# Norm factors return as broadcasts from DRAM instead of through transposes and matmuls on TensorE

## The chip, the core and the metric

The kernel runs on one core of one Trainium2 chip. A core has five engines with a queue of instructions each: TensorE (PE in the profile, its weight loads as PEld), VectorE (DVE), ScalarE (ACT), GpSimd (POOL) and SyncE (SP), which here issues almost all DMAs. Each engine runs its queue in order, and semaphores order the engines among themselves. PE reads SBUF and writes PSUM; a [128, 512] float32 tile of PSUM is one bank. The metric is the device time of one execution in microseconds. Times below come from the median of three timed runs and from one profiled execution.

## The reference

Two layers of a decoder trunk over 528 tokens (16 learned meta tokens, then 512), width 1024, batch 1, all in float32:

```python
for l in range(DEPTH):                                   # DEPTH = 2
    h = rmsnorm(h_res, norm_gain[l])
    proj = h @ w_in[l]
    u_pool, z_pool, c_q, c_kv, k_rope, z_mla, g_pool, g_mla = jnp.split(proj, IN_SPLIT_POINTS, axis=-1)
    y_pool = (pool_mix(u_pool, ...) * jax.nn.silu(z_pool)) @ pool_w_up[l]
    o_mla = mla(c_q, c_kv, k_rope, pos, ...)
    y_mla = (o_mla * jax.nn.silu(z_mla)) @ mla_w_up[l]
    merged = jax.nn.sigmoid(g_pool) * y_pool + jax.nn.sigmoid(g_mla) * y_mla
    h_res = h_res + merged @ w_out[l]
return h_res[:, N_META:]
```

`rmsnorm` divides each token's vector by the root of its mean square plus 1e-6. Inside `mla` the latents `c_q` (768 wide) and `c_kv` (256) are normalized in this way, then the queries and keys of 8 heads (96 wide, of which 32 are rotary) are computed from them, normalized per head and token, and used in causal softmax attention. Three sets of norm factors matter here: one per token for the residual stream, one per token for `c_kv`, and eight per token (one a head) for the keys.

## The kernel before

**Layout.** Tokens lie along the free dimension: an activation is a set of [128 features, 528 tokens] tiles. A norm factor, one number per token, must multiply all 128 partitions of such a tile, so it is needed as a [128, 528] tile with equal rows. The norms are applied late: the residual stream is multiplied by its gain and used as it is, and what leaves a projection is multiplied by the token's factor when it is evicted from PSUM.

**Products.** Each float32 product is made of three passes: operands are split into a rounded part (`hi`, float32r) and the rest (`lo`), and `mm3` (L179) issues hi x hi, hi x lo and lo x hi. Weights come in chunks of [128, 512]: `wload` (L165) loads one into a `raw` buffer from SP, ACT rounds it into `whi` (L175) and DVE subtracts it into `wlo` (L176). There are three buffers each of `raw`, `whi` and `wlo`, so a load waits until an earlier chunk has been converted, and a conversion until PE has used an earlier one.

**Order.** All weight products of both layers stand in one list, `plan`, made by `register` (L911). `stream` (L187) is a generator that emits them in this order, a few matmuls at a time, with an estimated cost. `go` (L977) writes the rest of the layer by hand and draws from this stream in between: `up(name)` emits until a product is done, `fill_now(ns)` (L264) emits products worth so many estimated ns. In the attention heads, `gap` (L974) does the same between scores, softmax and value products until a reserve is reached, so that PE always has independent products to work on. A scheduler then fixes each engine's order; PSUM tiles of the tag `mm` rotate through four banks.

**The start.** ACT issues the load of the first weight chunk; SP issues the gains, then x in five parts with three weight chunks between (L122 to L125), then the constants and the positions. PE runs ten matmuls on a tile of ones (L138). `split_h` (L329) makes `hh` and `hl` of a 128-feature slice of x, `square_x` (L336) its squares; the first projections `ckv0` and `ckv1` run over the slices as they come.

**Token norms.** `norm_sums` (L340) sums the squares of x and of `c_kv` over the partitions by matmuls with ones (L348), transposes the sums so that tokens lie along the partitions (L360, L361) and computes the inverse roots by three Newton steps on DVE (`newton`, L283) into `ninv`, [128, 2, 5]: factor, then four blocks of 128 tokens and one of the meta tokens. To come back along the free dimension, the factors are split in a rounded part and a rest and padded into a tile `v`; `rows` (L387) transposes it block by block on PE (L389, L391, L392) and ACT copies it out of PSUM into `kinv`; `spread` (L273) multiplies it with a selector, which sums the two parts and copies the row to 128 partitions (L276), and ACT copies the result into `self.inv` and `self.cinv`. The first is used by the evictions of `u`, `zp`, `zm`, `gp`, `gm` and of the rotary key, the second by those of the keys `k0` to `k3`.

**Key norms.** `qk_stats` (L638) does the same with the sums of squares of queries and keys, 16 per token: transposes (L657, L658), Newton into `ny` [128, 5, 16], then for two groups of four heads padding, `rows` (five transposes and two copies) and a DMA of four rows to DRAM (`kdr`, L685). `spread_k` (L692) loads a row back as a broadcast to 128 partitions (`bc`, three buffers). `prep` (L696) multiplies the keys of a head by it on DVE and POOL (L703, L704) and splits the product into `kh` and `kl` on ACT and DVE (L270, L271), which the scores of `head` (L717) read.

Of the kernel before, what the change touches and what calls it, by code (L numbers as in the profile page):

```python
# [9 lines left out]
F32 = mybir.dt.float32  # L10
F32R = mybir.dt.float32r
# [46 lines left out]
WARM = 10  # L58
# [13 lines left out]
def trunk(ctx, tc, xT, pos, win, wkr, wqb, wkb, wvb, wgr, wpu, wmu, wout, gains, const, yT):  # L72
# [26 lines left out]
    def mmt():  # L99
        return pp.tile([P, 512], F32, tag="mm", name=nm("mm"), bufs=4)  # L100
# [12 lines left out]
    def fetch(src, n, raw, eng):  # L113
        eng.dma_start(raw[:, :n], src)
        return raw

    def rawt():
        return wp.tile([P, 512], F32, tag="raw", name=nm("raw"), bufs=3)

    early.append(fetch(win[0, MT_CKV, :, 0:512], 512, slot("rinv"), act))  # L120
    sp.dma_start(gn, gains)
    for k0, k1, m, c in ((0, 1, 1, 0), (1, 2, None, 0), (2, 4, 0, 1), (4, 6, 1, 1), (6, 8, None, 0)):  # L122
        sp.dma_start(xb[:, k0:k1, :T], xT[:, k0:k1, :])
        if m is not None:
            early.append(fetch(win[0, MT_CKV + m, :, 512 * c:512 * c + 512], 512, rawt(), sp))  # L125
    xt = [xb[:, k] for k in range(8)]
    sp.dma_start(cst, const)
# [4 lines left out]
    sp.dma_start(posb[:, :T], pos.partition_broadcast(P))  # L132
# [8 lines left out]
    dve.tensor_copy(maskw[:, 512 - P:], cst[:, C_MASK:C_MASK + P])  # L141
    kinv = cp.tile([34, T], F32R, name="kinv")
    sel = cp.tile([64, 2], F32R, name="sel")
    gp.memset(sel.bitcast(F32), 0.0)
    for i in range(2):
        gp.memset(sel[32 * i:32 * i + 2, i:i + 1].bitcast(F32), 1.0)
    identr = cp.tile([P, P], F32R, name="identr")
    dve.tensor_copy(identr, ident)
# [30 lines left out]
    def mm3(out, wh, wl, xh, xl, start, stop):  # L179
        pe.matmul(out, wh, xh, start=start, stop=False)  # L180
        pe.matmul(out, wh, xl, start=False, stop=False)  # L181
        pe.matmul(out, wl, xh, start=False, stop=stop)  # L182

    plan = []
# [88 lines left out]
    def spread(dst, i):  # L273
        for a, b in FULL:
            ps = mmt()[:, :b - a]
            pe.matmul(ps, sel[0:34, i:i + 1].to_broadcast([34, P]), kinv[:, a:b], start=True, stop=True)  # L276
            act.activation(dst[:, a:b], ps, AF.Copy)

# [28 lines left out]
    kdr = [[dp.tile([4, T], F32, name=f"kdr{l}{s}") for s in range(2)] for l in range(DEPTH)]  # L307
# [3 lines left out]
    class Layer:  # L311
        def __init__(self, l):
            self.l, self.last = l, l == DEPTH - 1
            self.XS = XTOK if self.last else FULL
            self.x0 = NM if self.last else 0
            self.xt = xt if l == 0 else [None] * 8
            self.hs, self.us, self.zps = hbuf, [None] * 4, [None] * 4
            self.cs, self.cqs, self.ys, self.am = [None] * 2, [None] * 6, [None] * 4, [None] * 8
            self.kn, self.qn, self.zms, self.ogs = [None] * 4, [None] * 4, [None] * 4, [None] * 4
            self.qr, self.qf = [None] * 2, [None] * 2  # L320
            self.gms, self.mg, self.xr, self.vw = [None] * 8, [None] * 8, [None] * 8, []
            self.csq, self.xsq = [None] * 2, [None] * 8
            self.sq, self.nsq, self.asq = [], [0, 0], 0
            self.st = self.acc = self.inv = self.cinv = self.kraw = self.kp = None
# [4 lines left out]
        def split_h(self, k):  # L329
            gk, x = self.g(G_H + k), self.xt[k]  # L330
            hh, hl = self.hs[k]
            act.activation(hh[:, :T], x[:, :T], AF.Copy, scale=gk)
            dve.scalar_tensor_tensor(out=hl[:, :T], in0=x[:, :T], scalar=gk, in1=hh[:, :T].bitcast(F32),
                                     op0=ALU.mult, op1=ALU.subtract)

        def square_x(self, k):  # L336
            self.xsq[k] = slot(f"cq{4 + k}" if k < 4 else f"q{k}")
            act.activation(self.xsq[k][:, :T], self.xt[k][:, :T], AF.Square)

        def norm_sums(self):  # L340
# [30 lines left out]
            w = tmp()  # L371
            gp.memset(w[:, 0:170], 0.0)
            v = w[:, 0:170].rearrange("p (j c) -> p j c", c=34)
            nv = ny.rearrange("p a j -> p j a")
            nh = sm.tile([P, 5, 2], F32R, tag="nh", name=nm("nh"))
            dve.tensor_copy(nh, nv)
            dve.tensor_copy(v[:, :, 0:33:32], nh.bitcast(F32))
            dve.tensor_sub(v[:, :, 1:34:32], nv, nh.bitcast(F32))
# [8 lines left out]
        def rows(self, v, n, out):  # L387
            kt1, kt2 = mmt(), mmt()
            pe.transpose(kt1[0:n, 0:NM], v[0:NM, 4, :], ident[0:NM, 0:NM])  # L389
            for j in range(3):  # L390
                pe.transpose(kt1[0:n, NM + P * j:NM + P * (j + 1)], v[:, j, :], ident)  # L391
            pe.transpose(kt2[0:n, 0:P], v[:, 3, :], ident)  # L392
            c1 = NM + 3 * P
            act.activation(out[0:n, 0:c1], kt1[0:n, 0:c1], AF.Copy)
            act.activation(out[0:n, c1:T], kt2[0:n, 0:P], AF.Copy)
# [242 lines left out]
        def qk_stats(self):  # L638
# [35 lines left out]
            ws = []  # L674
            for s in range(2):
                w = tmp()
                gp.memset(w, 0.0)
                v = w[:, 0:485].rearrange("p (j c) -> p j c", c=97)
                dve.tensor_copy(v[:, :, 0:97:32], ny[:, :, 4 * s:4 * s + 4])
                ws.append(v)  # L680
# [11 lines left out]
        def spread_k(self, h):  # L692
            self.bcs[h] = bc = slot("bc", bufs=3)
            sp.dma_start(bc, kdr[self.l][h // 4][h % 4:h % 4 + 1, :].partition_broadcast(P))
# [216 lines left out]
        def register(self, nxt):  # L911
# [17 lines left out]
            for m in range(3):  # L929
                cq(m)  # L930
# [11 lines left out]
            cq(3)  # L942
# [8 lines left out]
            cq(4)  # L951
            y(3)
            cq(5)
# [23 lines left out]
        def go(self, nxt):  # L977
            l = self.l
            up = lambda name: upto((l, name))
            if l == 0:  # L980
                for k in range(8):
                    if k in (0, 1, 3, 5):
                        step()
                    self.split_h(k)
            up("ckv1")
# [4 lines left out]
            up("u0")  # L990
# [7 lines left out]
            up("cq3")  # L998
# [7 lines left out]
            fill_now(2600)  # L1006
            kq = self.prep(0)
            fill_now(2600)
# [102 lines left out]
```

## Time and profile before

| | us |
|---|---|
| median of 3 runs | 802.42 |
| lowest, highest | 802.06, 803.46 |
| the profiled execution | 803.0 |
| its span, first to last instruction | 801.2 |
| PE busy | 793.5 |
| DVE busy | 527.8 |
| ACT busy | 417.0 |
| POOL busy | 196.2 |

A row of a timeline has the start in us from the span's start, the time in us, the engine, the source line, the operation, out<-in by the program's names, the shape and the count of like instructions merged, and in brackets idle time of the engine and what ended it. The chain of waits has start, length and what; its shares say where the chain that ended last was. Matmuls are pipelined, so that one takes longer than the distance to the next; their starts show the rate. In the view of waits a row has the waiting instruction, what it waited for, us in total, how often and the longest. In the table of queues a row has packets, MB and the time that the packets took as a share of 16 DMA engines over the stretch.

### The profile page before, as it was taken

The numbers are of one execution on the slowest core, as the hardware profiler recorded it, in microseconds if no ns is written. First come the engines' busy times: TensorE is split into PE (matmuls) and PEld (weight loads), VectorE is DVE, ScalarE is ACT, GpSimd is POOL, SyncE is SP. The second block draws the span as 40 slices with busy tenths as digits, with TensorE's granted clock in tenths as the row PEclk, the third lists the DMA queues.
The fourth block names the chain that finished last, engine by engine and source line by source line (L and its number), as shares of the span: only waits on it lengthen the run. The fifth ranks groups of instructions, "written<-read, shape, count | busy, mean of one in ns | idle before, by whom it ended". The sixth has DMA issues, their size and how long they took to land.

```text
span 801.2 us, 14644 instructions
## 1 busy us (share of the span) xinstructions
PE 793.5 (99%) x5343; PEld 715.1 (89%) x5343; DVE 527.8 (66%) x1139; ACT 417.0 (52%) x946; POOL 196.2 (24%) x266
## 2 busy tenths in 40 slices
PE   9999999999999999999999999999999999999998
PEld 8889999999999999999997897877788888887887
DVE  5568767437689887685354686665467889664942
ACT  7455645545556665543254456445455666644421
POOL 1024404103433322142000164032024333410600
PEclk9999999999999999999999999999999999999999
DMA  6222233324222222224642222324242322222272
GB/s 240 73 64 96 73 100 91 109 83 140 86 87 87 78 69 67 83 89 143 181 142 73 73 87 86 98 81 119 85 157 90 101 84 79 68 78 69 92 227 102
DMA packets 48872, 80.71 MB, mean 101 GB/s; under 512 B 5904, under 2 KB 14480, under 8 KB 48800
## 3 DMA queue, kind: packets, MB, share of 16 engines
q1 hardware_dynamic: 48656, 79.52, 32.3%
q8 instruction: 42, 0.69, 0.4%
q14 instruction: 30, 0.25, 0.1%
q10 hardware_dynamic: 144, 0.26, 0.1%
HBM read 73.40 MB, written 4.23 MB: 97 GB/s over the span
## 4 chain that ended last, share of the span: by engine, by line
PE 95%; DMA 2%; ACT 1%; DVE 1%; issue 0%; POOL 0%; SPq 0%; ACTq 0%; POOLq 0%
PE mm L180 28%; PE mm L182 27%; PE mm L181 27%; PE mm L798 2%; PE S L180 2%; PE S L181 2%; PE S L182 2%; PE o L804 1%; PE o L803 1%; PE mm L348 1%; PE S L457 1%; DMA raw<-wmu 1%; DMA xb<-xT 1%; DMA bc<-kdr 1%; PE mm L415 0%
## 5 line engine op out<-in xcount | busy, mean ns | idle before, releaser
L180 PE MATMUL mm<-hh,whi 128*128 128x264 f32 (+2 forms) x1096 | 346.3, 318 | 0.2 <-ACT racc L812 0.2
L181 PE MATMUL mm<-hl,whi 128*128 128x264 f32 (+2 forms) x1096 | 343.5, 314 | 0.0
L182 PE MATMUL mm<-hh,wlo 128*128 128x264 f32 (+2 forms) x1096 | 342.2, 315 | 0.0
L176 DVE TENSOR_TENSOR wlo<-raw,whi 128x512 fp32r<-128x512 f32 (+2 forms) x251 | 186.5, 747 | 120.1 <-ACT whi L175 112.6
L175 ACT ACTIVATE whi<-raw 128x512 fp32r<-128x512 f32 (+2 forms) x251 | 150.3, 602 | 185.9 <-PE mm L181 131.5
L180 PEld LDWEIGHTS mm<-hh,whi 128*128 128x128 f32 x1096 | 205.7, 188 | 13.5 <-ACT racc L812 0.5
L181 PEld LDWEIGHTS mm<-hl,whi 128*128 128x128 f32 x1096 | 206.2, 188 | 12.2 <-issue 0.4
L182 PEld LDWEIGHTS mm<-hh,wlo 128*128 128x128 f32 x1096 | 205.1, 188 | 12.7 <-issue 0.4
L704 POOL TENSOR_TENSOR tmp<-kp,bc 64x528 f32<-64x528 f32 x16 | 24.5, 1531 | 113.5 <-DMA bc<-kdr 78.2
L535 POOL TENSOR_TENSOR racc<-racc,tmp 128x264 f32<-128x264 f32 (+1 forms) x15 | 14.1, 942 | 143.5 <-ACT tmp L534 143.4
L776 POOL TENSOR_TENSOR pm<-pa,rs 128x16 f32<-128x16 f32 x32 | 11.6, 361 | 145.5 <-DVE rs L771 140.7
L886 POOL TENSOR_TENSOR tmp<-tmp,xb 128x264 f32<-128x264 f32 (+1 forms) x24 | 27.0, 1145 | 59.1 <-DVE tmp L884 33.7
L732 DVE CUSTOM_DVE_ANT_0 S<-S,maskw,nqs 128x272 f32<-128x272 f32 (+4 forms) x80 | 38.4, 498 | 1.6 <-PE S L182 1.2
L739 ACT ACTIVATE cq<-S,bia 128x400 f32<-128x400 f32 (+2 forms) x48 | 24.6, 516 | 21.5 <-DVE bia L766 11.6
L180 PE MATMUL mm<-u,whi 128*128 128x264 f32 (+1 forms) x108 | 35.3, 327 | 0.0
L182 PE MATMUL mm<-cq,wlo 128*128 128x264 f32 (+1 forms) x108 | 34.8, 323 | 0.0
L182 PE MATMUL mm<-u,wlo 128*128 128x264 f32 (+1 forms) x108 | 34.8, 322 | 0.0
L181 PE MATMUL mm<-cq,whi 128*128 128x264 f32 (+1 forms) x108 | 34.8, 322 | 0.0
L180 PE MATMUL mm<-cq,whi 128*128 128x264 f32 (+1 forms) x108 | 34.7, 322 | 0.0
L271 DVE TENSOR_TENSOR tl<-mm,th 128x512 fp32r<-128x512 f32 (+1 forms) x64 | 29.3, 481 | 6.8 <-ACT th L270 5.8
L778 POOL TENSOR_TENSOR cq<-cq,rs 128x384 f32<-128x384 f32 (+1 forms) x32 | 32.8, 1025 | 0.0
L180 PE MATMUL mm<-q,whi 128*128 128x264 f32 (+1 forms) x96 | 30.0, 324 | 1.0 <-ACT whi L175 0.5
(262 smaller groups left out, 1380.0 us busy)
## 6 DMA issues: line engine op xcount, KB each, us to landing
raw<-win SPq DMA_DIRECT2D x143, 256.0 KB, 2.6
raw<-wout SPq DMA_DIRECT2D x32, 256.0 KB, 3.1
bc<-kdr SPq DMA_DIRECT2D x16, 264.0 KB, 3.6
raw<-wpu SPq DMA_DIRECT2D x16, 256.0 KB, 2.7
raw<-wmu SPq DMA_DIRECT2D x16, 256.0 KB, 2.6
raw<-wqb SPq DMA_DIRECT2D x12, 256.0 KB, 2.7
tmp<-xT SPq DMA_DIRECT2D x16, 132.0 KB, 2.9
tmp<-scr SPq DMA_DIRECT2D x7, 256.0 KB, 4.7
```

The costliest lines, as they stand in the source:

```text
L175: act.activation(hi[:, :n], raw[:, :n], AF.Copy)
L176: dve.tensor_sub(lo[:, :n], raw[:, :n], hi[:, :n].bitcast(F32))
L180: pe.matmul(out, wh, xh, start=start, stop=False)
L181: pe.matmul(out, wh, xl, start=False, stop=False)
L182: pe.matmul(out, wl, xh, start=False, stop=stop)
L271: dve.tensor_sub(lo[:, a:b], src, hi[:, a:b].bitcast(F32))
L704: gp.tensor_mul(kf[r0:r0 + 64, :], self.kp[r0:r0 + 64, :], bc[r0:r0 + 64, :])
L732: dve.tensor_tensor_reduce(out=sv, in0=sv, in1=mask, scale=nqs[:, i, h:h + 1], scalar=3e38, op0=ALU.add, op1=ALU.min, accum_out=bia[:, c:c ...
L739: act.activation(pv, sv, AF.Exp, scale=-1.0, bias=bia[:, i:i + 1], accum_out=rs[:, c:c + 1])
L778: gp.tensor_mul(pt[i][:, NM:], pt[i][:, NM:], rs[:, i:i + 1].to_broadcast([P, n - NM]))
L798: pe.transpose(tr[:, P * (i - j):P * (i - j + 1)], pt[i][:, NM + P * j:NM + P * (j + 1)], ident)
L886: gp.tensor_add(t[:, :b - a], t[:, :b - a], self.am[m][:, a:b])
```

## The change

The factors leave the layout in which Newton makes them (tokens along the partitions) by DMAs that write them one element at a time into DRAM rows, `ndr` for the two token norms and `kdr` for the keys, and come back by a load that copies a row to 128 partitions. `rows`, `spread`, `kinv`, `sel` and the padding go. The load back is tied to a product: `behind` adds a wait for `newest`, the last matmul emitted by `mm3` at that point. `cq3` and `cq4` move ahead of `u0`, `cinv` gets another slot, `up("u0")` goes, `up("cq3")` becomes `up("k3")`, and the amounts of `fill_now` change. At the start, the loads of x from the third slice on, with weights between, constants and positions, wait for the landing of the first weight chunk; the first `split_h` works in halves; in layer 0 the squares of a slice wait until the slice three later has been rounded; there are eight warm-up matmuls.

```diff
-WARM = 10
+RET = 12500.0
+WARM = 8
...
-    early.append(fetch(win[0, MT_CKV, :, 0:512], 512, slot("rinv"), act))
+    early.append(slot("rinv"))
+    first = act.dma_start(early[0][:, 0:512], win[0, MT_CKV, :, 0:512])
     sp.dma_start(gn, gains)
-    for k0, k1, m, c in ((0, 1, 1, 0), (1, 2, None, 0), (2, 4, 0, 1), (4, 6, 1, 1), (6, 8, None, 0)):
-        sp.dma_start(xb[:, k0:k1, :T], xT[:, k0:k1, :])
-        if m is not None:
-            early.append(fetch(win[0, MT_CKV + m, :, 512 * c:512 * c + 512], 512, rawt(), sp))
+    sp.dma_start(xb[:, 0, :T], xT[:, 0, :])
+    early.append(fetch(win[0, MT_CKV + 1, :, 0:512], 512, rawt(), sp))
+    sp.dma_start(xb[:, 1, :T], xT[:, 1, :])
...
+    def other_loads(made):
+        for k, m in ((2, 0), (4, 1), (6, None)):
+            ins = sp.dma_start(xb[:, k:k + 2, :T], xT[:, k:k + 2, :])
+            behind(ins, made)
+            if m is not None:
+                raw = rawt()
+                behind(sp.dma_start(raw, win[0, MT_CKV + m, :, 512:1024]), made)
+                early.append(raw)
+        behind(sp.dma_start(cst, const), made)
+        behind(sp.dma_start(posb[:, :T], pos.partition_broadcast(P)), made)
...
     def mm3(out, wh, wl, xh, xl, start, stop):
...
-        pe.matmul(out, wl, xh, start=False, stop=stop)
+        newest[0] = pe.matmul(out, wl, xh, start=False, stop=stop)
...
-    def spread(dst, i):
-        for a, b in FULL:
-            ps = mmt()[:, :b - a]
-            pe.matmul(ps, sel[0:34, i:i + 1].to_broadcast([34, P]), kinv[:, a:b], start=True, stop=True)
-            act.activation(dst[:, a:b], ps, AF.Copy)
...
-    kdr = [[dp.tile([4, T], F32, name=f"kdr{l}{s}") for s in range(2)] for l in range(DEPTH)]
+    ndr = [[dp.tile([1, T], F32, name=f"ndr{l}{i}") for i in range(2)] for l in range(DEPTH)]
+    kdr = [dp.tile([H, T], F32, name=f"kdr{l}") for l in range(DEPTH)]
...
         def square_x(self, k):
...
+            if self.l == 0:
+                behind(made, self.made[min(k + 3, 7)])
...
             newton(ny, na, nt)
-            w = tmp()
-            gp.memset(w[:, 0:170], 0.0)
...
-            fill_now(8200)
-            self.rows(v, 34, kinv)
-            self.inv, self.cinv = slot("rinv"), slot("cq9")
-            fill_now(1300)
-            spread(self.inv, 0)
-            spread(self.cinv, 1)
+            self.inv, self.cinv = slot("rinv"), slot("q1")
+            for i, d in enumerate((self.inv, self.cinv)):
+                row = ndr[self.l][i]
+                sp.dma_start(row[0, NM:T].rearrange("(j p) -> p j", p=P), ny[:, i, 0:4])
+                sp.dma_start(row[0, 0:NM].rearrange("(p j) -> p j", j=1), ny[0:NM, i, 4:5])
+            fill_now(RET)
+            for i, d in enumerate((self.inv, self.cinv)):
+                behind(sp.dma_start(d[:, 0:T], ndr[self.l][i].partition_broadcast(P)), newest[0])
...
-            fill_now(9500)
-            for s, v in enumerate(ws):
-                t = tmp()
-                self.rows(v, 97, t[0:97, 0:T])
-                sp.dma_start(kdr[self.l][s], t[0:97:32, 0:T])
+            row = kdr[self.l]
+            for j in range(4):
+                sp.dma_start(row[:, NM + P * j:NM + P * (j + 1)].rearrange("h p -> p h"), ny[:, j, 0:8])
+            sp.dma_start(row[:, 0:NM].rearrange("h p -> p h"), ny[0:NM, 4, 0:8])
+            fill_now(11000)
             self.bcs = {}
             for h in range(2):
-                self.spread_k(h)
+                behind(self.spread_k(h), newest[0])
...
-            for m in range(3):
+            for m in range(5):
                 cq(m)
...
             self.norm_sums()
-            up("u0")
...
-            up("cq3")
+            up("k3")
             self.mix(3)
...
             self.qk_stats()
-            fill_now(2600)
+            fill_now(3600)
             kq = self.prep(0)
-            fill_now(2600)
+            fill_now(3600)
```

More of the change, by code (lines that the diff above doesn't have):

```diff
@@ L140, in trunk @@
     gp.memset(maskw[:, :512 - P], 0.0)
[L141 to L146, printed above, removed]
-    identr = cp.tile([P, P], F32R, name="identr")
-    dve.tensor_copy(identr, ident)
+    identr = cp.tile([P, P], F32R, name="identr")
+    def other_loads(made):
[8 more added lines that the diff above has]
+        behind(sp.dma_start(posb[:, :T], pos.partition_broadcast(P)), made)
+        dve.tensor_copy(maskw[:, 512 - P:], cst[:, C_MASK:C_MASK + P])
+        dve.tensor_copy(identr, ident)
     tcos = cp.tile([P, T], F32, name="tcos")
@@ L321, in __init__ @@
             self.gms, self.mg, self.xr, self.vw = [None] * 8, [None] * 8, [None] * 8, []
+            self.made = [None] * 8
             self.csq, self.xsq = [None] * 2, [None] * 8
@@ L693, in spread_k @@
             self.bcs[h] = bc = slot("bc", bufs=3)
-            sp.dma_start(bc, kdr[self.l][h // 4][h % 4:h % 4 + 1, :].partition_broadcast(P))
+            return sp.dma_start(bc, kdr[self.l][h:h + 1, :].partition_broadcast(P))
         def prep(self, h):
@@ L950, in register @@
             y(2)
-            cq(4)
+            cq(5)
             y(3)
-            cq(5)
             for r in range(2):
@@ L984, in go @@
                     self.split_h(k)
+                    if k == 0:
+                        other_loads(first)
             up("ckv1")
```

36 lines of the change are left out of this document (7 added, 29 removed).

## Prediction

> **What bounds the kernel now.** I read the page first: who is busy, and which engine carries the chain that ended last.
>
> ```profile
> PE 793.5 (99%) x5343; PEld 715.1 (89%) x5343; DVE 527.8 (66%) x1139; ACT 417.0 (52%) x946; POOL 196.2 (24%) x266
> PEclk9999999999999999999999999999999999999999
> PE 95%; DMA 2%; ACT 1%; DVE 1%; issue 0%; POOL 0%; SPq 0%; ACTq 0%; POOLq 0%
> ```
>
> TensorE (PE) is busy 99% of the span at full granted clock and is 95% of the chain. Since "busy" is modelled, I checked the view of waits for PE alone: its longest waits are these, each once.
>
> ```profile
> PE S L180 <- ACT kh L270: 0.6, 1, 0.6
> PE mm L276 <- ACT rinv L277: 0.5, 1, 0.5
> PE S L180 <- ACT hh L332: 0.4, 1, 0.4
> ```
>
> So the time is the sum of what PE issues plus a few waits under 1 us. Any instruction taken off PE shortens the end by its issue pitch, and a new wait of PE lengthens it one for one. Work on DVE, ACT, POOL and SP counts only where PE ends up waiting for it. This is the state in which the change has to be priced.
>
> **Part 1, what leaves PE.** The change drops 30 transposes (six calls of `rows`, five each), eight matmuls of `spread`, and two of ten warm-up matmuls. Pipelined matmuls are priced by start to start, not by their duration. The timeline of PE around the layer-0 norm rows:
>
> ```profile
> 40.41 0.28 PE L181 MATMUL mm<-hl,whi 128*128 128x264 f32 x1
> 40.53 0.28 PE L182 MATMUL mm<-hh,wlo 128*128 128x264 f32 x1
> 40.74 0.19 PE L389 MATMUL mm<-cst,tmp 16*34 16x16 f32 x1
> 40.85 0.50 PE L391 MATMUL mm<-cst,tmp 128*34 128x128 f32 x3
> 41.20 0.27 PE L392 MATMUL mm<-cst,tmp 128*34 128x128 f32 x1
> 41.22 0.37 PE L180 MATMUL mm<-hh,whi 128*128 128x264 f32 x1
> 41.43 0.28 PE L181 MATMUL mm<-hl,whi 128*128 128x264 f32 x1
> ...
> 42.28 0.28 PE L182 MATMUL mm<-hh,wlo 128*128 128x264 f32 x1
> 42.49 0.63 PE L276 MATMUL mm<-kinv,sel 34*128 34x264 f32 x3
> 43.60 0.38 PE L276 MATMUL mm<-kinv,sel 34*128 34x264 f32 x1 [0.48 <-ACT rinv L277]
> 43.91 0.39 PE L180 MATMUL mm<-hh,whi 128*128 128x264 f32 x1
> 44.14 0.28 PE L181 MATMUL mm<-hl,whi 128*128 128x264 f32 x1
> ```
>
> An ordinary 264-column matmul starts every 0.12 us (40.41 to 40.53). From 40.53 to 41.43 there would be two pitches (0.24) without the rows; it takes 0.90, so a group of five costs 0.66, the slow matmuls on both sides included. The four spreads take 44.14 - 42.28 - 0.24 = 1.62, of which 0.48 is the wait for ACT to empty a PSUM bank. The other groups by their outer rows, on the same timeline:
>
> ```profile
> 174.60 0.28 PE L182 MATMUL mm<-u,wlo 128*128 128x264 f32 x1
> ...
> 175.53 0.28 PE L181 MATMUL mm<-th,whi 128*128 128x264 f32 x1
> ...
> 176.04 0.37 PE L182 MATMUL mm<-u,wlo 128*128 128x264 f32 x1
> ...
> 177.28 0.28 PE L181 MATMUL mm<-th,whi 128*128 128x264 f32 x1
> ```
>
> ```profile
> 450.10 0.28 PE L181 MATMUL mm<-hl,whi 128*128 128x264 f32 x1
> ...
> 450.98 0.29 PE L180 MATMUL mm<-hh,whi 128*128 128x264 f32 x1
> ```
>
> ```profile
> 577.36 0.40 PE L182 MATMUL mm<-u,wlo 128*128 128x512 f32 x1
> ...
> 578.63 0.39 PE L181 MATMUL mm<-th,whi 128*128 128x512 f32 x1
> ```
>
> Key rows of layer 0: 0.93 - 0.24 = 0.69 and 1.24 - 0.24 = 1.00. Layer 1's matmuls are 512 wide, pitch 0.12 x 512/264 = 0.23, so one of its two key groups costs 1.27 - 0.46 = 0.81, both 1.62. Its norm rows I take as layer 0's, 0.66. One pair of its spreads costs 0.88 - 0.24 = 0.64, both pairs 1.28. Sum: 0.66 + 1.69 + 1.62 + 0.66 + 1.62 + 1.28 = **7.5 us**. Nothing covers this work today, PE issues it in line; the ACT and DVE copies around it are off the path and I price them at nothing.
>
> **Part 2, the return of the key norms, where the change can lose.** The chain of waits shows how keys return now:
>
> ```profile
> 177.03 1.72 DMA kdr<-tmp
> 178.77 4.78 DMA bc<-kdr
> 183.71 1.77 POOL tmp L704
> 185.50 0.65 ACT kh L270
> 186.20 0.57 PE S L180 x2
> ```
>
> From issue of the broadcast to the first scores takes 186.20 - 178.77 = 7.4 us. In the changed program the factors are written straight from their [128, 8] layout: four DMAs of 1,024 single elements and one of 128, 4,224 in all, 264 on each of 16 DMA engines. The broadcasts stand behind them on SP, waiting for their landing and for one named matmul. Let T0 be the end of the transposes of the statistics (L657/L658):
>
> ```profile
> 165.00 0.17 PE L658 MATMUL mm<-cst,tmp 16*16 16x16 f32 x1
> ```
>
> ```profile
> 169.42 0.24 DVE L290 SCALAR_TENSOR_TENSOR ny<-nt,ny 128x80 f32<-128x80 f32 x1
> ```
>
> So the factors exist 169.66 - 165.00 = 4.7 us after T0. By the changed program's order, 89 matmuls lie between T0 and the matmul that the broadcast waits for (10.7 us) and 73 more before the first scores (8.8 us, T0 + 19.5). In layer 1 it is 47 and 39 wide ones, 10.9 and 9.1 us. If the writes have landed by T0 + 10.7, kh is ready at T0 + 18.1: 1.4 us to spare, and the 0.6 us that PE waits for kh today, before the first scores (first row of the view of waits), is gone. I book **0.6 us** of gain. PE stalls only if the writes land after T0 + 12.1, which is 7.4 us after the first is issued.
>
> What does a one-element write cost? No row here shows one. The lower bound is nothing beyond today's small store, 1.72 us from issue to landing. Above, the page's queue row gives the mean packet of the kernel, mostly 2 KB long:
>
> ```profile
> q1 hardware_dynamic: 48656, 79.52, 32.3%
> ```
>
> 0.323 x 801.2 x 16 / 48,656 = 85 ns. The nearest row is the same view for the first 2.2 us, where hardly more than the 192-byte rows of the gains move on that queue:
>
> ```profile
> q1 hardware_dynamic: 58, 0.01, 3.1%
> ```
>
> 0.031 x 2.2 x 16 / 58 = 19 ns. I take 19: 264 x 19 = 5.0 us, landing 6.7 us after issue, within the 7.4; the far end, 85 ns, is 22.4 us and a stall of 22.4 + 1.7 - 7.4 = 16.7 us in each layer. So this part is 0 with little room, and the bounds are 0 and +33 us. The Trainium skill, "DMA: Bandwidth & Descriptors", Rules for kernel authors, speaks against the change: a strided last dimension becomes one descriptor per element and should be rearranged. Its section Bandwidth gives about 10.5 ns a packet; by that the estimate would be 2.8 us of engine time and the sum would stay as it is. No run here shows either yet.
>
> **Part 3, the norm return.** Only 1,056 elements in four DMAs, 66 per engine: 1.3 us at 19 ns. In layer 0 the broadcast waits for the matmul 94 pitches (11.3 us) behind its transposes, Newton included; the first reader that could hold PE (u0's eviction, whose PSUM is needed again by u1) is 139 matmuls or 16.7 us later, against 4.8 us for a broadcast. Moving cq3 and cq4 ahead of u0 makes that room. So nothing. On SP both broadcasts stand ahead of weight loads; but the first load behind them waits itself for a buffer that a later matmul frees, so the wait delays no load as long as the writes are in time. `fill_now` takes 11,000 before, and 3,600 twice in place of 2,600 around, the first head, so the heads have about 3 us less filler left; in the built order the filler still lasts into the last head in both layers. I allow **-0.3 us** for small waits at those ends.
>
> **Part 4, the start.** The first matmuls:
>
> ```profile
> 1.05 4.64 PE L138 MATMUL wps<-ones 128*128 128x128 f32 x20 [1.05 <-DVE na L662]
> ```
>
> ```profile
> 5.34 0.79 PE L180 MATMUL S<-hh,whi 128*128 128x264 f32 x2
> ```
>
> ```profile
> 2.12 5.04 DMA xb<-xT
> 7.17 0.74 ACT hh L332
> 7.96 0.51 PE S L180 x2
> ```
>
> Warm-up ends where real work starts, so eight instead of ten and a halved first split let it start up to 0.5 us sooner. The second slice of x lands at 7.16 because three more loads share the engines; the change holds these back until the first weight has landed, so it should come about 1 us earlier. But the third and fourth slice are then issued only after that landing, and PE needs them 24 matmuls (2.9 us) on. Bounds: gain 1.2, loss 0.5; I take **0.5 us** of gain, since the same bytes have to arrive before the same point.
>
> **Sum.** 7.5 + 0.6 + 0 - 0.3 + 0.5 = 8.3 us off. The profiled execution took 803.0 us (span 801.2 and 1.8 around it), 0.6 above the median of 802.42. Its forecast is 794.7, and against the median **794.1 us**.
>
> **Rivals.**
> A. *Slow element writes* (the other side). If a one-element write costs far more than 19 ns, through the write side of DRAM or the making of descriptors, the broadcasts land late; POOL, ACT and the first scores of each layer wait, and PE in order behind them. It decides from (8.3/2 + 7.4 - 1.7)/264 = 37 ns: there the two stalls of 4.2 us eat the whole gain; at 60 ns each stall is 60 x 264 / 1000 + 1.7 - 7.4 = 10.1 us, time 794.1 + 20 = 814. For it: PE has nothing but 7.4 us to cover the writes, and the kernel's mean packet takes 85 ns. Against it: the nearest small packets take 19. The rule of the Trainium skill named in part 2 is of this kind.
> B. *Part of it given back*: 21 to 37 ns per element, stalls of up to 4 us per layer, 795 to 802.
> C. *The change gains only the PE work that it removes*: the later x slices cost what the earlier start gives or more, the bigger filler uses come back as waits in the last heads. Worth 0.6 + 0.5 - (-0.5) and some tenths: 795.5 to 797.
> D. That the transposes do not leave PE is excluded: the built program has 40 fewer PE instructions, 5,173 matmuls instead of 5,213.
>
> **How the numbers follow.** Forecast with its small errors (792 to 795.4) 0.56, C 0.12, B 0.12, A 0.20 (of which 0.03 falls within 0.2% of before). A measurement of this kernel tells 0.2%, 1.6 us, from no change. Faster: 0.56 + 0.12 + 0.10 = 0.78; same 0.05; slower 0.17. The range 791.8 to 800.5 leaves out A, the end of B and a few hundredths below.
>
> **What would show it.** In the profile after: PE instructions 40 fewer and the span shorter by about their pitch; no L276 or L389 to L392; in the view of waits, the 0.6 us before the first scores gone and no wait for kh or the broadcast above 1 us in either layer; the landing of the broadcast of keys at 3 to 5 us; the key writes landed within 7.4 us of the first issue; the first real matmul before 5.0 us and PE steady from 9 us on. I am wrong if PE waits several us for the POOL or DVE product of the key broadcast at the first head of each layer, if SP sits on the broadcast while weight conversions starve, or if PE idles longer before the fourth slice of x than it does now.

## The result, and the profile after

The changed kernel takes 836.0 us (median of four, 830.5 to 839.1) against 802.2 us for the kernel before, measured with it: ratio 1.041, 95% interval 1.039 to 1.043. It is slower by 34 us where 8 us less were forecast. The profiled execution is the shortest of the four, 830.5 us with a span of 828.7.

The page of the changed kernel, rows in the order of those shown of before (busy engines, PE and its granted clock in 40 slices of 20.7 us, the chain's shares):

```profile
PE 791.4 (95%) x5301; PEld 713.3 (86%) x5301; DVE 532.0 (64%) x1130; ACT 410.0 (49%) x927; POOL 197.3 (24%) x257
PE   9999899992999999999999999999949999999998
PEclk9999999996999999999999999999969999999999
PE 84%; DMA 8%; DVE 3%; issue 1%; POOL 1%; ACT 1%; SPq 1%; DVEq 0%; ACTq 0%; POOLq 0%
```

PE issues 42 instructions fewer, as it should: 30 transposes, eight matmuls of `spread` and two warm-up matmuls, each of which the page counts twice (x20 for ten before). But it now has two holes, slices 10 and 30, just ahead of the first head of each layer, and DMA's share of the chain goes from 2% to 8%. The view of waits names what PE waited for (total, times, longest):

```profile
PE mm L186 <- ACT xb L533: 14.1, 1, 14.1
PE mm L186 <- ACT whi L181: 7.6, 1, 7.6
PE S L186 <- ACT kh L277: 5.1, 2, 4.3
PE mm L186 <- DVE vt L574: 2.8, 1, 2.8
PE mm L186 <- DVE u L467: 1.7, 1, 1.7
```

The two largest are not the scores (S). They are ordinary filler matmuls, one waiting for ACT to empty a PSUM bank (L533), one for a weight conversion (L181). What held ACT stands on its timeline in layer 0, and what held that on the timeline of SP's DMA issues:

```profile
180.36 0.39 ACT L533 ACTIVATE xb<-mm 128x264 f32<-128x264 f32 x1 [0.68 <-PE mm L188]
199.30 0.63 ACT L181 ACTIVATE whi<-raw 128x512 fp32r<-128x512 f32 x1 [18.55 <-DMA raw<-win]
199.83 0.37 ACT L533 ACTIVATE xb<-mm 128x264 f32<-128x264 f32 x1
```

```profile
172.92 2.25 SPq L667 DMA_DIRECT2D kdr<-ny  x4
175.21 10.53 SPq L668 DMA_DIRECT2D kdr<-ny  x1
185.84 0.85 SPq L115 DMA_DIRECT2D raw<-win  x2
198.37 1.28 SPq L678 DMA_DIRECT2D bc<-kdr  x3
```

The fifth key write, of 128 elements, keeps SP for 10.5 us. That it stands behind the four before it is a reading of this row; with the same writes spaced apart, in a run below, it takes 0.7 us. The weight loads behind it go out 10 us late and then lie behind the elements; ACT can begin on the first at 199.3. ACT takes its work in order and stands idle for 18.6 us ahead of that conversion, so the finished bank that PE needs, which comes behind it, is emptied only at 199.8: PE waits 14.1 us for it. The broadcasts start only when the elements have landed, 25.4 us after the first issue. The chain shows the second route, behind the first:

```profile
175.21 23.09 DMA kdr<-ny
198.37 4.20 DMA bc<-kdr
202.71 2.37 POOL tmp L688
205.11 0.65 ACT kh L277
```

The DMA view, cut to the time of the first 3 us and of the 22.4 us that follow, has one row each for SP's queue (packets, MB, share of 16 engines):

```profile
q1 hardware_dynamic: 2491, 0.18, 90.6%
```

```profile
q1 hardware_dynamic: 2146, 0.45, 122.6%
```

In the first stretch a packet takes 0.906 x 3.0 x 16 / 2,491 = 17 ns, close to the 19 that the prediction took. In the second it takes 1.226 x 22.4 x 16 / 2,146 = 205 ns; since the share is above 100%, packets of one engine overlap there, and this is the time of a packet, not the distance between two. Over half of the elements are taken up at once; then the rest crawl. And once PE works again it does so at half clock for some microseconds (stretches of the same kernel: start and end, length, busy time and count of PE, PEld, DVE, ACT and POOL, then the granted clock, the DMA share and GB/s):

```profile
186.00:200.00 14.00, 0.17 (x2) 0.00 (x0) 0.00 (x0) 0.70 (x2) 0.00 (x0) 0.68 1.04 36
200.00:205.00 5.00, 4.49 (x18) 4.05 (x18) 1.30 (x2) 0.20 (x1) 2.29 (x1) 0.52 0.56 219
205.00:210.00 5.00, 3.93 (x30) 3.55 (x30) 3.96 (x11) 3.08 (x8) 0.08 (x1) 1.00 0.67 181
```

On PE's timeline just after the hole the pitch of a 264-column matmul is 0.22 us:

```profile
200.86 0.42 PE L188 MATMUL mm<-hh,wlo 128*128 128x264 f32 x1
201.08 0.42 PE L186 MATMUL mm<-hh,whi 128*128 128x264 f32 x1
```

That makes the hole dearer than its length: 18 matmuls at 0.22 instead of 0.12 are 2 us. In layer 1, behind holes of 7.6 and 4.3 us, the clock reads 0.50 and 0.52 for 10 us. The Trainium skill, "TensorE: Matmul & The Clock Gate", section "Part 1: The HAM clock gate", gives half rate after an idle window of about 3.4 us; the 0.52 after 14 us of idling agrees.

### The profile page after: what moved, and what is told of

Its sections match the earlier page's. It is cut to its first block, busy times and chain, and to the rows that moved or that the text cites. A ratio compares the mean times of both kernels' runs of the same rounds, so it can differ in the third digit from the quotient of the medians.

```text
span 828.7 us, 14522 instructions
## 1 busy us (share of the span) xinstructions
PE 791.4 (95%) x5301; PEld 713.3 (86%) x5301; DVE 532.0 (64%) x1130; ACT 410.0 (49%) x927; POOL 197.3 (24%) x257
## 4 chain that ended last, share of the span: by engine, by line
PE 84%; DMA 8%; DVE 3%; issue 1%; POOL 1%; ACT 1%; SPq 1%; DVEq 0%; ACTq 0%; POOLq 0%
PE mm L186 24%; PE mm L188 24%; PE mm L187 24%; DMA kdr<-ny 5%; PE mm L782 2%; PE S L187 2%; PE S L188 1%; PE S L186 1%; PE o L788 1%; DMA raw<-win 1%; PE o L787 1%; PE mm L355 1%; DMA bc<-kdr 1%; PE S L448 1%; DVE wlo L182 1%
## 5 line engine op out<-in xcount | busy, mean ns | idle before, releaser
L186 PE MATMUL mm<-hh,whi 128*128 128x264 f32 (+2 forms) x1096 | 348.2, 319 | 24.0 <-ACT xb L533 14.1
L181 ACT ACTIVATE whi<-raw 128x512 fp32r<-128x512 f32 (+2 forms) x251 | 150.6, 602 | 221.2 <-PE mm L187 137.0
L760 POOL TENSOR_TENSOR pm<-pa,rs 128x16 f32<-128x16 f32 x32 | 9.8, 308 | 155.7 <-DVE rs L755 155.7
L716 DVE CUSTOM_DVE_ANT_0 S<-S,maskw,nqs 128x400 f32<-128x400 f32 (+4 forms) x80 | 38.4, 496 | 3.8 <-PE S L188 3.6
L687 DVE TENSOR_TENSOR tmp<-kn,bc 64x528 f32<-64x528 f32 x16 | 13.1, 816 | 39.9 <-DMA bc<-kdr 39.7
```

Source lines behind the costliest of these rows:

```text
L181: act.activation(hi[:, :n], raw[:, :n], AF.Copy)
L716: dve.tensor_tensor_reduce(out=sv, in0=sv, in1=mask, scale=nqs[:, i, h:h + 1], scalar=3e38, op0=ALU.add, op1=ALU.min, accum_out=bia[:, c:c ...
```

## The experiments

Two theories to start with. *Stuck queue*: the writes drain slowly, and everything behind them on SP is late, the filler's own weights first. *Late broadcast*: only who reads the elements is late. Each time is set against runs of the kernel before on the same chip (801.5 to 801.8 us).

### The parts, one at a time

Start alone, put into the kernel before (the change's own lines: held-back loads, split in halves, order of squares, WARM 8):

```diff
-    early.append(fetch(win[0, MT_CKV, :, 0:512], 512, slot("rinv"), act))
+    early.append(slot("rinv"))
+    first = act.dma_start(early[0][:, 0:512], win[0, MT_CKV, :, 0:512])
...
+                    if k == 0:
+                        other_loads(first)
```

> The kernel before with the changed start alone (held-back loads, first split in halves, eight warm-up matmuls). In the changed kernel the norm sums of layer 0 begin at 24.20 us, in the kernel before at 24.96: if this is all the start's doing and nothing is given back, 0.76 us off, 801.6. If the later slices of x only move the wait, no change, 802.4. More than 1 us either way would speak against both.

Measured 801.4 us, ratio 0.9995 (0.9986 to 1.0004): a gain of 0.4 us that the measurement can't tell from none. Norm sums of layer 0 begin at 24.4 us instead of 25.0. Nothing of the loss is here.

Keys as before (and the fills 9500 and 2600), norms through DRAM:

```diff
-            for j in range(4):
-                sp.dma_start(row[:, NM + P * j:NM + P * (j + 1)].rearrange("h p -> p h"), ny[:, j, 0:8])
+                self.rows(v, 97, t[0:97, 0:T])
+                sp.dma_start(kdr[self.l][s], t[0:97:32, 0:T])
```

> The changed kernel with the keys' factors returned as before (transposes into rows, two small stores, fills as before); the norm factors still go to DRAM one by one. Theory 'stuck queue' (element writes leave slowly, and the weight loads queued behind them on SP hold ACT and then PE): the two large stalls of 14 and 8 us and the slow clock after them are gone, the wait of 1.7 us after the norm of layer 0 stays: 802.4 - 4.2 (PE work of the norm rows and spreads) - 0.8 (start) + 1.7 to 3 = 798 to 800.5. Rival 'norm writes are free': 797.2. Rival 'the loss is not in the keys': above 815.

Measured 802.2 us, ratio 1.0003 (0.9994 to 1.0012). The two holes are gone: the keys' return makes 836.0 - 802.2 = 34 us. But the norms' return, with 4.2 us of PE work less, gains nothing, and its waits say why:

```profile
PE mm L186 <- DVE vt L584: 2.8, 1, 2.8
PE mm L186 <- DVE u L477: 1.4, 1, 1.4
```

2.8 + 1.4 = 4.2 us, as much as the whole gain. The expectation, 798 to 800.5, had the second wait only, and its upper end was 1.7 us too low.

Norms as before (rows, spreads, order of cq), keys through DRAM:

```diff
-            for m in range(5):
+            for m in range(3):
                 cq(m)
...
-            self.inv, self.cinv = slot("rinv"), slot("q1")
+            self.rows(v, 34, kinv)
+            spread(self.inv, 0)
```

> The changed kernel with the norm factors returned as before (rows, spreads, order of the query projections as before); the keys' factors still go to DRAM one by one. Theory 'stuck queue': the stalls before the first head of each layer stay whole, 836 + 4.2 of norm work on PE - 2 to 3 of waits behind the norm = 837 to 838.5. If the two parts disturb each other (norm writes late, so that the filler runs out at the keys), it is far below: under 825.

Measured 830.8 us, ratio 1.036 (1.034 to 1.037): the holes stay, but the time is 6 to 8 us below what was expected. Norms through DRAM cost 5 us on top of the slow keys and about nothing without them. In layer 0 the hole is 11.1 us here, 14.1 in the changed kernel. But the two profiled executions, 831.4 and 830.5 us, don't differ by the 5 us of the medians, so no trace shows where they go; why the parts add up to more together wasn't tried further.

### Is it the reader that is late?

The kernel before, plus the 4,224 writes to a tile that nothing reads:

```diff
+            extra = kdx[self.l]
+            for j in range(4):
+                sp.dma_start(extra[:, NM + P * j:NM + P * (j + 1)].rearrange("h p -> p h"), ny[:, j, 0:8])
+            sp.dma_start(extra[:, 0:NM].rearrange("h p -> p h"), ny[0:NM, 4, 0:8])
             ws = []
```

> The kernel before, all as it was, plus the 4,224 single-element writes of the changed kernel at the same place on SP, to a DRAM tile that nothing reads. Theory 'stuck queue': the weight loads behind them stand still, ACT waits in a weight conversion, PE for the PSUM eviction behind it, and the key rows stored later land late too: 820 to 840. Rival 'late broadcast' (only who reads the elements is late): 802.4.

Measured 832.9 us, ratio 1.039 (1.037 to 1.041). SP shows the picture of the changed kernel, 9.5 us in the fifth write and the next weight loads behind it:

```profile
169.04 3.21 SPq L677 DMA_DIRECT2D kdx<-ny  x4
172.29 9.52 SPq L678 DMA_DIRECT2D kdx<-ny  x1
181.91 4.13 SPq L114 DMA_DIRECT2D raw<-win  x2
```

Nearly the whole loss, 31 of 34 us, comes from writes that no instruction waits for. "Late broadcast" falls as the main cause. PE does wait 3.9 us for kh in this run too, because the old stores of key rows stand behind the new writes on SP.

More filler ahead of the broadcasts:

```diff
-            fill_now(11000)
+            fill_now(24000)
```

> The changed kernel with 24,000 instead of 11,000 units of filler between the key writes and the broadcasts, so that 13 us more of PE work stand before the first heads. Rival 'late broadcast': with 13 us more cover most of both stalls is gone, below 812. Theory 'stuck queue': the filler itself needs the weight loads that stand behind the writes; the stalls of 14 and 8 us stay, only the 4 to 5 us of waiting for kh before the first scores go: 825 to 832.

Measured 842.2 us, ratio 1.051 (1.050 to 1.053): worse by 6 us than the changed kernel and outside both expectations. The waits for kh are gone, as expected, but the holes stay, 15.1 and 9.1 us, and the last heads, now without that filler, wait for ACT, DVE and POOL in pieces of up to 1.3 us. More filler doesn't cover the lateness; that it lives on the loads that are stuck fits the holes, which again end with ACT. My size was wrong: it counted the waits that go, not the filler that is missing later.

### Why do the writes drain so slowly?

A kernel that only moves the factors, form after form. In the first version only the first transfer of a form waited for the form before, so that forms overlapped, and it gave rates but no times:

> No layer is computed, the output is not the reference's: the kernel only moves one set of 8 x 528 factors over and over, each time in another form, and each form waits for the landing of the one before. Forms: single elements to dense DRAM as the changed kernel writes them (five times, once with a weight load of 256 KB behind on SP, once with one on ACT's queue), half as many, elements 64 B apart, 512 B apart, 32-byte runs (8 heads of a token), 128-byte runs (32 tokens), single-element reads from DRAM, single-element copies inside SBUF. Theory 'drain of element writes': dense elements take 20 to 25 us from first issue to landing with nothing beside them, half as many about half, copies inside SBUF and the runs under 8 us. Rival 'contention': alone they land in under 8 us, and what cost 25 us was the weight traffic beside them. Under the first, elements 64 B apart tell whether writes into one 64-byte line hold each other: if they do, the spaced form is at least twice as fast; if the count alone decides, all three spacings take the same. A weight load behind them on the same queue lands after them; on ACT's queue it lands within 4 us if the queue is what holds it, and late if the engines are.

Its five sets of dense elements each stretched over some 20 us with hardly any weight traffic beside them, while spaced elements, reads and copies inside SBUF passed quickly. So "contention" falls. The second version lets every transfer wait for all of the form before:

```diff
     def batch(pairs, eng=sp):
         ins = []
-        for n, (d, s) in enumerate(pairs):
-            m = sp.dma_start(d, s)
-            if n == 0:
-                for q in prev:
-                    behind(m, q)
+        for d, s in pairs:
+            m = eng.dma_start(d, s)
+            for q in prev:
+                behind(m, q)
             ins.append(m)
```

> No layer is computed. As the run of forms before it, but now every transfer of a form waits for all of the form before (there only the first one did, and forms overlapped). Added: elements 8 B and 32 B apart, so that a 64-byte line takes 8 or 2 of them instead of 16, and 'far apart': the dense 16.9 KB once more, but in 16 transfers of 264 elements of which no two share a 64-byte line, so that the 16 writes to one line lie half a microsecond from each other. Theory 'one line': writes that meet in one 64-byte line wait for each other. Then the time falls with the number per line, from 16 to 25 us dense to under 7 us from 64 B on, and the far-apart form lands soon after its last issue (9 us of issues, landed by 12). Rival 'small region': what counts is that 16.9 KB are few memory banks; then far apart takes as long as dense, 16 us or more, and the spaced forms get faster with the region they span, 512 B apart faster than 64 B. Rival 'count': all the same. The weight load 4 us behind the element writes: on SP's queue it lands with their end; on ACT's queue within 4 us of its issue if only the queue's order holds it.

SP's timeline: start of a form's first issue, time spent issuing, transfers. A form has landed when the next starts.

```profile
0.97 3.81 SPq L95 DMA_DIRECT2D densea<-ny  x5
26.32 3.92 SPq L95 DMA_DIRECT2D denseb<-ny  x5
50.57 2.56 SPq L95 DMA_DIRECT2D half<-ny  x5
63.94 2.86 SPq L95 DMA_DIRECT2D lineeight<-ny  x5
81.90 2.86 SPq L95 DMA_DIRECT2D linethirty<-ny  x5
89.94 2.86 SPq L95 DMA_DIRECT2D linesixty<-ny  x5
96.88 2.86 SPq L95 DMA_DIRECT2D linefive<-ny  x5
104.86 6.91 SPq L95 DMA_DIRECT2D farapart<-ny  x16
114.47 2.25 SPq L95 DMA_DIRECT2D token<-ny  x5
118.18 3.21 SPq L95 DMA_DIRECT2D run<-wt  x5
122.35 3.19 SPq L95 DMA_DIRECT2D rd<-densea  x5
127.43 2.87 SPq L95 DMA_DIRECT2D tosb<-ny  x4
132.34 0.40 SPq L95 DMA_DIRECT2D xb<-win  x1
134.91 3.42 SPq L95 DMA_DIRECT2D densec<-ny  x5
139.43 0.36 SPq L146 DMA_DIRECT2D densecraw<-win  x1
159.73 3.81 SPq L95 DMA_DIRECT2D densed<-ny  x5
```

By the differences of the first column: dense 25.3 and 24.2 us, half as many 13.4; 8 B apart 18.0; 32 B apart 8.0; 64 B apart 6.9; 512 B apart 8.0; reads 5.1; copies inside SBUF 4.9. The number of elements is the same in all but the half. So neither the count nor SBUF nor reading is slow: dense writing is. And the same dense 16.9 KB, written so that the neighbours of a 64-byte stretch lie in different transfers, issued 0.44 us apart (far apart; its source is 33 partitions instead of 128), takes 9.6 us, 6.9 of them issues. "Small region" falls with that, and "one line" stands, with the unit open: single elements that go to the same few tens of bytes of DRAM right behind one another hold each other. Runs of 8 heads (3.7 us) or 32 tokens (4.2 us, 3.2 of them issues) are done almost as they are issued.

The weight load alone took 2.6 us (132.34 to 134.91). Behind the elements on SP's queue it took 20.3 us (139.43 to 159.73). On ACT's queue it was issued at 164.21, and this is the DMA view of the 8 us after 164.0, with all queues that moved a packet:

```profile
q1 hardware_dynamic: 897, 0.00, 113.7%
```

Only SP's elements; ACT's 144 packets lie after 173 us. Another queue doesn't get past them: it is not the queue's order alone that holds the load. The Trainium skill, "DMA: Bandwidth & Descriptors", section "Issuing engines are not separate DMA queues", says that DMAs of all issuing engines run on the same 16 DMA engines; this agrees.

Does that hold inside the kernel? The run of before with writes that nobody reads, but 512 B apart:

```diff
-                sp.dma_start(extra[:, NM + P * j:NM + P * (j + 1)].rearrange("h p -> p h"), ny[:, j, 0:8])
+                sp.dma_start(extra[:, NM + P * j:NM + P * (j + 1), 0].rearrange("h p -> p h"), ny[:, j, 0:8])
...
+    kdx = [dp.tile([H, T, 128], F32, name=f"kdx{l}") for l in range(DEPTH)]
```

> The kernel before plus 4,224 single-element writes that nobody reads, as in the run that took 832.9 us, but each 512 B from the next. If the count of descriptors is what costs, as the rule of one descriptor per element has it, again 825 or more; if the writes hold each other only where they are dense, they land within 6 us and the weight loads behind them are little late: 801.5 to 806.

Measured 802.7 us, ratio 1.0013 (1.0004 to 1.0022). The same number of element writes costs 1.1 us in place of 31. SP's issues of the four and of the fifth:

```profile
168.82 2.55 SPq L677 DMA_DIRECT2D kdx<-ny  x4
171.41 0.71 SPq L678 DMA_DIRECT2D kdx<-ny  x1
```

And the changed kernel with its own dense writes in another order:

```diff
-            for j in range(4):
-                sp.dma_start(row[:, NM + P * j:NM + P * (j + 1)].rearrange("h p -> p h"), ny[:, j, 0:8])
+            for r in range(4):
+                for j in range(4):
+                    part = row[:, NM + P * j:NM + P * (j + 1)].rearrange("h (q r) -> r q h", r=4)
+                    sp.dma_start(part[r], ny[r:P:4, j, 0:8])
```

> The changed kernel with the same 4,224 single-element writes of key factors to the same places, but in 16 transfers of every fourth token instead of four of all tokens (and the 16 meta tokens as they were), so that only 4 instead of 16 writes to a 64-byte line follow each other at once and the next four come 1.8 us later. SP needs some 7.5 us for 17 issues instead of 2.9. Theory 'one line': the writes land about 2 us after the last issue, 9 to 10 us after the first, 2 to 3 us later than the cover of 7.4 us: some 5 to 8 us of stalls in all on top of the 802.2 of the version with keys as before less its 4 us of PE work for the keys: 803 to 808. Theory 'count' or 'small region': the drain of 20 us stays, 830 or more.

Measured 817.4 us, ratio 1.019 (1.018 to 1.021), between the expectations of both theories. The same elements in the same places, in another order and in more transfers, give back 19 of the 34 us, so order and pace matter. But the 16 issues took 11.7 us, not 7:

```profile
173.25 11.68 SPq L669 DMA_DIRECT2D kdr<-ny  x16
195.03 1.28 SPq L680 DMA_DIRECT2D bc<-kdr  x3
```

and the broadcast could start only 21.8 us after the first. The weight loads behind the writes went out at 185.7 us, as late as in the changed kernel (185.8), now because of the issues. So this run doesn't tell whether four neighbours at once still hold each other or SP's issues make the rest of the loss; 2 or 1 in this kernel weren't tried.

### The same change without single elements

VectorE transposes the factors in 32x32 blocks, and DRAM gets runs of 32 tokens: 136 writes for the keys, 34 for the norms. The rest is the changed kernel.

```diff
+            w, wt = [sm.tile([P, 64], F32, tag=t, name=nm(t)) for t in ("kw", "kwt")]
+            dve.memset(w, 0.0)
+            dve.tensor_copy(w[:, 0:40].rearrange("p (j h) -> p j h", j=5), ny[:, :, 0:8])
+            dve.transpose(wt, w)
             row = kdr[self.l]
-            for j in range(4):
-                sp.dma_start(row[:, NM + P * j:NM + P * (j + 1)].rearrange("h p -> p h"), ny[:, j, 0:8])
+            for b in range(4):
+                sp.dma_start(row[:, NM:T].rearrange("h (j b q) -> b j h q", j=4, b=4)[b], wt[32 * b:32 * b + 32, 0:32])
```

> The changed kernel with its factors transposed in 32x32 blocks on VectorE before they are written, so that DRAM gets runs of 32 tokens: 136 writes instead of 4,224 for the keys, 34 instead of 1,056 for the norms, same route otherwise, no transposes on PE. Theory 'the number of element writes': everything else of the change is as forecast, so the time is the sum of the prediction, 794.1, at most 797 with VectorE's three extra operations in each chain; no wait of PE above 1 us. Rival 'the way over DRAM itself is too long for the cover': stalls of several us before the first heads stay, 805 or more.

Measured 795.0 us against 801.8, ratio 0.992 (0.990 to 0.993): the change gives 6.8 of the 8.3 us that it was priced at once its writes are runs. One wait above 1 us is left, which is not of the writes:

```profile
PE mm L186 <- DVE vt L579: 2.8, 1, 2.8
```

It is also in the run with keys as before, and in neither run with the old order of cq. In the kernel before, cq3 stands between k3 and v; with cq3 and cq4 moved ahead of u0, the evictions of v fall on VectorE's and ACT's part of the pooling mixes. So one of them goes back (and RET goes from 12,500 to 11,000, which isn't separated from it):

```diff
-            for m in range(5):
+            for m in range(4):
                 cq(m)
...
+            cq(4)
             add("v", wvb[l], 1024, body=self.v_body)
```

> The version with runs of 32 tokens, and the query projection cq4 put back between k3 and v (four instead of five ahead of u0), so that the evictions of v do not fall on the pooling mixes: the wait of 2.8 us of PE for VectorE in v goes. If nothing else moves: 795.0 - 2.8 = 792.2. If the norm factors then come too late for u0: 795 or more, with a wait of PE at u0's eviction.

Measured 793.3 us against 801.5, ratio 0.990 (0.988 to 0.991), 8.3 us faster than the kernel before, some 42 us faster than the changed one, and 1.1 us above the 792.2 that was expected. The wait in v shrank to 0.5; a new one of 0.8 (L530) took part of it.

```profile
PE mm L186 <- ACT tmp L530: 0.8, 1, 0.8
PE mm L186 <- DVE vt L579: 0.5, 2, 0.3
```

## Why the prediction was wrong

*What bounds the kernel.* Right: PE's idle time came out one for one. The view of waits after adds to 31 us in its five rows; with 2 us of slow clock in layer 0, and more of it in layer 1, less the 8 us of gain, it is close to the 27.5 us by which the profiled execution is longer.

*Part 1, 7.5 us less on PE.* Borne out with the sum that it is the main term of, by the version with runs and cq4 back: 8.3 us less than before in place of the forecast 8.3, with all PE work gone that the change takes away. That the two agree to the tenth is chance, since the interval reaches from 6.9 to 9.5 us; no run measures part 1 by itself.

*Part 2, the step that failed*: "What does a one-element write cost? ... I take 19: 264 x 19 = 5.0 us, landing 6.7 us after issue". The landing came 25.4 us after the first issue, 25.4 / 264 = 96 ns per element and engine. The first 2,491 packets of the stretch did take 17 ns each. But the row that the 19 came from moves the gains, 192-byte rows that are loaded into SBUF; it is a read, and reads of single elements are fast here as well (5.1 us). It says nothing of single elements that are written side by side into DRAM. The far end of my bounds, a stall of 16.7 us per layer, was near the truth (the keys' return cost 34 us in all), but by luck: it came from 85 ns, the mean of packets of mostly 2 KB, and the stalls took another way than the one priced. Rival A had the side. I gave it 0.20 because of the one cheap row against it, and that row was of another kind of transfer.

Two more steps of part 2 were too narrow. The arrow of the wait: I let the writes be late only for the broadcast, POOL and the first scores; they are late first for the weight loads behind them on SP, then for ACT's conversion, then for the bank behind it in ACT's order, then for PE. I asked what is queued behind the wait for the norms alone, and only for writes in time. One of my signs of being wrong did name starving weight conversions, but no bound priced them. And the slow clock after a long hole, some 2 us in layer 0, stood in no bound. The 0.6 us booked for kh did come once the writes were runs: no wait for kh is left there.

The rule that I weighed, from the Trainium skill, "DMA: Bandwidth & Descriptors", section "Rules for kernel authors" (a strided last dimension becomes one descriptor per element), pointed the right way, but its count is not the cost here: the same count 512 B apart cost 1.1 us. The 10.5 ns a packet that the Trainium skill gives in "DMA: Bandwidth & Descriptors", section "Bandwidth", I misused: there it is the 0.67 us of one 4 KB load issued from GpSimd, shared among its 64 packets, not the time of a write on one of 16 engines. A rule of the Trainium skill that I did not weigh stands in "VectorE: DVE Perf Modes", section "The three transpose paths": a plain strided DMA copy used as a transpose is given as 19 times slower than the DMA's own transpose when the destination's inner stride is large. No run here used that transpose; against runs of 32 tokens the strided copy was 25.3 / 4.2 = 6 times slower. A large stride by itself isn't what cost here, since elements 512 B apart took 8.0 us.

*Part 3, "So nothing".* Wrong by 4.2 us, the whole PE gain of the norms. The element writes landed 7.7 to 8.5 us after issue, not in 1.3 plus the way (rows of the changed kernel, KB each and median us from issue to landing):

```profile
ndr<-ny SPq DMA_DIRECT2D x4, 2.0 KB, 8.5
ndr<-ny SPq DMA_DIRECT2D x4, 0.1 KB, 7.7
```

PE waited 1.4 us for u0's eviction (1.7 in the changed kernel), but not because the factors were late. In the version with keys as before their broadcasts went out at 43.7 and 45.1 us and landed within 6.3 us; the eviction came at 61.1. What was late was weights again, as its chain shows:

```profile
38.56 8.84 DMA raw<-win
58.03 2.05 DMA raw<-wkr
```

The first load behind the element writes took 8.8 us, ACT and VectorE fell behind, and in VectorE's order the eviction came after work on `wkr`, whose load went out at 58.0 instead of 53.8 in the version with runs. So the condition "as long as the writes are in time" failed, and with runs, where ACT waits for no load at this place, the wait is gone. The other 2.8 us are the cover that I did not name: I asked what the moved cq3 and cq4 hide ahead of u0, not what they had hidden where they stood. The allowance of 0.3 us for small waits at the heads' ends can't be told apart in these runs.

*Part 4, 0.5 us.* Not contradicted: 0.4 us, within what can't be measured.

*Rivals.* A came true in its place and side, at 25 us of drain for 4,224 elements, 96 ns per element and engine, where 37 was the point from which it decides. Of its two mechanisms the write side of DRAM fits; "the making of descriptors" does not, since the same number of spaced writes is cheap. B and C are out, D as well. (C's own sum, 0.6 + 0.5 + 0.5, gives 795.7 as its lower end, not 795.5; nothing hangs on it.)

## What to carry to other kernels

Price a DMA by its landing under the pattern that it will have (direction, run length, neighbours in flight), not by the time of a packet of another kind; where no row of the profile has that pattern, the far bound deserves the weight. Then follow the queue: everything issued behind a slow transfer is late, also on other issuing engines, and the first victim can be work that has nothing to do with it. To turn a [128, n] column of factors into rows in DRAM, transpose 32x32 on VectorE first and write runs; and when a matmul group is moved to cover one thing, ask what it covered where it stood.

## What the runs showed of the hardware

Single 4-byte writes to DRAM took 25 us for 4,224 when transfers wrote all 16 elements of a 64-byte stretch right behind one another, 18 us with 8 elements to a stretch, 8 us with 2, and 7 us with one; reads and copies inside SBUF took 5. Whether the unit is 64 bytes, and whether the memory or the way to it does the holding, these runs don't show. Behind such a backlog a load issued on ACT's queue moved no packet for 8.8 us. And the granted clock was 0.52 in the 5 us after a hole of 14 us of PE, then 1.00.
